# A two-block network in float32 on one core: six edits at waits of TensorE

## The chip, the cores and the metric

The kernel runs on one core of a Trainium2 chip. The metric is the device time of one execution in microseconds, the median over repeated runs. One execution was also taken with the hardware profiler; its rows give the time of every instruction on the five engines: TensorE (PE in the profile; PEld is its weight load), VectorE (DVE), ScalarE (ACT), GpSimd (POOL) and SyncE (SP, which issues most transfers).

## The reference, cut to what matters

The input is 512 tokens of 1024 features. Two hybrid layers come first, then a second block with a state space branch (S5) and a pooling branch, then a final norm. All is float32.

```
def l2norm(t):
    return tf * rsqrt(sum(tf * tf, -1) + EPS)              # q and k of the delta net, 8 heads of 128

# one hybrid layer
h = rmsnorm(x, pre_mix_g);  proj = h @ w_in                # splits: dn_q,k,v,z,b,a, sw_q,k,v, gate_a, gate_b
o = gated_delta_rule(l2norm(q) / sqrt(128), l2norm(k), v, g, beta)   # chunks of 64
y_a = (rmsnorm(o, norm_g) * silu(z)) @ w_up_dn
probs = softmax over a window of 128 keys (with sinks);  o = probs @ v    # 16 query, 2 key/value heads of 64
y_b = o @ w_up_sw
x = x + rmsnorm((sigmoid(gate_a) * y_a + sigmoid(gate_b) * y_b) @ w_o, post_mix_g)
ff = square(relu(rmsnorm(x, pre_mlp_g) @ w_ff1)) @ w_ff2   # 1024 -> 4096 -> 1024
x = x + rmsnorm(ff, post_mlp_g)

# S5 branch of the second block: 32 groups of 16 channels, 64 complex states
dt = exp(log_dt);  abar = exp(lam * dt);  bbar = (abar - 1) / lam * b
s_t = abar * s_(t-1) + bbar u_t;  y = re(c s) + d * u
```

## The kernel before

**Products.** A product with a weight matrix takes 128 output features at a time. The weight tile comes from HBM as `raw` (128x8x128, 512 KB), is rounded to a high part `wh` (ScalarE, L221 and L241; GpSimd for some, L239), and VectorE subtracts to get the low part `wl` (L222, L242). The activations are split in the same way (`split`, L333 to L340: names such as xsh and xsl, ah, hh and hl). Each tile is three matmuls per 128 rows of the contraction, high by high, high by low, low by high (`mm3`, L245; the call itself is L78, a transposition L81). A tile of all 512 tokens is 24 such matmuls. `wh` and `wl` have three buffers, `raw` two; `keep` tiles `kw` have their own pool. PSUM tiles are `psm` (three) and `psa` (five).

**Order.** The program is written as generators that are stepped by `hop()` and `rest()`, and a scheduler then orders the instructions of each engine by its own estimate of times; what is given to `keep_in_program_order` stays in the written order. Each engine works through its own list in order, so an instruction that waits holds all behind it. SP's list holds nearly all loads and stores; the two first `tz` tiles of the second block are loaded by ScalarE's queue (L1572).

**Stages of a layer** (layer 0 in the profile's time, layer 1 some 980 us later). Projections, the convolution and sliding attention, up to 240 us: `sw_item` (L927) exponentiates the scores, transposes them, ScalarE copies them to `pc` (L1007), GpSimd makes two masked copies, `pv` for the block before and `pc` for the own block (L1010, L1012), and TensorE multiplies each by its block of `vt`. The delta net, to 470 us; `norms` (L634) squares four heads of q or k (`sqk`) and TensorE sums over the 128 features of a head, with the squares as the stationary operand and one column of ones moving. The gates and the two up projections, 470 to 580 us (L1303 to L1350): per tile n, `ogf` and two or three gates are fetched from HBM into one ring of three tiles, tag "fe" (L1313); VectorE multiplies ogf by gate 0 (L1335), splits it to `ah`, and multiplies the product of the up projection by gate 2 into `tb` (L1340). `w_o`, to 635 us. FF, 635 to 950 us, in four groups of 1024 hidden features: `relu2` (L1377) makes ft, fq, hh and hl from PSUM or, for the tiles that `fast_pair` forms, from y; `ssm_tables` (L1046) is stepped beside it and makes the S5 tables: it loads `row`, `dt`, `lbr`, `lbi` and `crow` in small pieces (L1059 to L1105). The last group's down projection (L1479 to L1490) works on half the tokens at a time and keeps its last five weights as `kw`.

**Second block,** from 2000 us: TensorE transposes u, ScalarE copies it to `uab` (L1585), TensorE transposes again for `u_g`; then `xv` (L1607), a complex product, scan and complex product on VectorE (L1029 to L1034, L1612) to `sv`, and the products that read sv with `wt`.

Of the kernel before, what the change touches and what calls it, by code (L numbers as in the profile page):

```python
# [9 lines left out]
F32 = mybir.dt.float32  # L10
# [4 lines left out]
ALU = mybir.AluOpType  # L15
# [4 lines left out]
P = 128  # L20
SEQ = 512
D = 1024
NB = SEQ // P
KD = D // P
# [10 lines left out]
EPS = 1e-6  # L35
# [19 lines left out]
def body(  # L55
# [10 lines left out]
    V, S, G, DMA = nc.vector, nc.scalar, nc.gpsimd, nc.sync  # L66
# [33 lines left out]
    def rest(n):  # L100
        for _ in range(n):
            yield
# [17 lines left out]
    def ps_ax(shape=(P, 4, P), name="psa"):  # L120
        return pp.tile(list(shape), F32, tag="ax", name=name, bufs=5)
# [34 lines left out]
    def t2(name, shape=(P, SEQ), dtype=F32):  # L156
        return tp.tile(list(shape), dtype, tag="t2", name=name, bufs=NT2)
# [64 lines left out]
            V.tensor_tensor(out=lo, in0=t, in1=f32(h), op=ALU.subtract)  # L222
            return h, lo

    def load_w(src, kn=KD, n=P, pool_h=False, keep=None):
        turn[0] += 1
        if turn[0] % 3 == 2 and turn[1] is not None and turn[0] > turn[2]:
            raw = turn[1].tile([P, kn, n], F32, tag="rawx", name="rawx", bufs=1)
        else:
            raw = wp.tile([P, kn, n], F32, tag="raw", name="raw", bufs=2)  # L230
        DMA.dma_start(out=raw, in_=src.rearrange("(k p) n -> p k n", p=P))
        h = lo = None
        if keep is not None:
            h, lo = keep(kn, n), keep(kn, n)
        if h is None:
            h = wp.tile([P, kn, n], F32R, tag="wh", name="wh", bufs=3)
            lo = wp.tile([P, kn, n], F32R, tag="wl", name="wl", bufs=3)
        if pool_h:
            G.tensor_scalar(out=h, in0=raw, scalar1=1.0, scalar2=0.0, op0=ALU.mult, op1=ALU.add)  # L239
        else:  # L240
            S.copy(out=h, in_=raw)  # L241
        V.tensor_tensor(out=lo, in0=raw, in1=f32(h), op=ALU.subtract)  # L242
        return h, lo

# [359 lines left out]
    class Quad:  # L604
# [29 lines left out]
        def norms(s, src):  # L634
            sq = [t2("sqk") for _ in range(4)]
            for hh in range(4):
                S.activation(out=sq[hh], in_=src[:, hh].rearrange("p b t -> p (b t)"), func=AF.Square)
            yield from rest(NRM)
            ps = ps_ax((P, NB, 4))
            for hh in range(4):  # L640
                for b in range(NB):
                    T.matmul(ps[:, b, hh:hh + 1], lhsT=sq[hh][:, b * P:(b + 1) * P], rhs=ones[:, 0:1], start=True, stop=True)
                if hh == 1:
                    yield
            ss = small((P, NB, 4), "ss", 2)
            V.tensor_scalar(out=ss, in0=ps, scalar1=EPS, scalar2=None, op0=ALU.add)
            nr = small((P, NB, 4), "nr", 2)
            G.tensor_tensor(out=nr, in0=ss, in1=mhalf.rearrange("p (b h) -> p b h", h=4), op=ALU.pow)
            return ss, nr
# [277 lines left out]
    def sw_item(l, b, kv, qk, vt, sw, kts, db):  # L927
# [70 lines left out]
        V.reciprocal(out=den, in_=den)  # L998
        V.tensor_tensor(out=sc, in0=sc, in1=den.unsqueeze(3).to_broadcast([P, 2, 4, P]), op=ALU.mult)
        yield from rest(PRB)  # L1000
        pcs = []
        for o in range(2):
            ps = ps_ax()
            for i in range(4):
                T.transpose(ps[:, i, :], sc[:, o, i, :], ident)
            pc, pv = sw.tile([P, 4, P], F32, tag="pc", name="pc", bufs=2), None
            S.copy(out=pc, in_=ps)  # L1007
            if b:
                pv = sw.tile([P, 4, P], F32, tag="pv", name="pv", bufs=2)
                G.affine_select(out=pv, in_=pc, pattern=[[0, 4], [-1, P]], base=0, channel_multiplier=1,  # L1010
                                compare_op=ALU.is_gt, fill=0.0)
            G.affine_select(out=pc, in_=pc, pattern=[[0, 4], [1, P]], base=0, channel_multiplier=-1,  # L1012
                            compare_op=ALU.is_ge, fill=0.0)
            pcs.append((pc, pv))
        yield from rest(PV)
        po = ps_ax()
        for o, (pc, pv) in enumerate(pcs):
            hs = slice(64 * o, 64 * o + 64)
            dst = po[hs].rearrange("p h t -> p (h t)")
            if b:  # L1020
                T.matmul(dst, lhsT=vt[:, b - 1, kv * 64:kv * 64 + 64], rhs=pv.rearrange("p h t -> p (h t)"), start=True, stop=False)
            T.matmul(dst, lhsT=vt[:, b, kv * 64:kv * 64 + 64], rhs=pc.rearrange("p h t -> p (h t)"), start=not b, stop=True)
        of = r2("sof")
        V.tensor_copy(out=of, in_=po)
        DMA.dma_start(out=db[:, 4 * kv:4 * kv + 4, b * P:(b + 1) * P], in_=of)
# [20 lines left out]
    def ssm_tables(sp, hf):  # L1046
# [6 lines left out]

        prs = slice(NG * hf, NG * hf + NG)
        grs = slice(2 * NG * hf, 2 * NG * hf + 2 * NG)
        lam = {}
        for nm, src in (("lr", ssm_lam_re_2), ("li", ssm_lam_im_2)):
            row = sp.tile([NG, P], F32, tag="row", name="row")
            DMA.dma_start(out=row, in_=src[0, grs].rearrange("(i two) p -> i (two p)", two=2))  # L1059
            ps = ps_ax((P, NG))  # L1060
            T.transpose(ps, row, ident[:NG, :NG])
            lam[nm] = tl(nm)
            V.tensor_copy(out=lam[nm], in_=ps)
        lr, li = lam["lr"], lam["li"]
        dt = tl("dt")
        for half in range(2):
            DMA.dma_start(out=dt[64 * half:64 * half + 64, :],
                          in_=ssm_log_dt_2[0, grs].rearrange("(i two) -> two i", two=2)[half].partition_broadcast(64))
        bre, bim = tl("lbr", (P, NG, 2, 16))[:, :, 0, :], tl("lbi", (P, NG, 2, 16))[:, :, 0, :]
        for dst, src in ((bre, ssm_b_re_2), (bim, ssm_b_im_2)):  # L1070
            for half in range(2):
                DMA.dma_start(out=dst[64 * half:64 * half + 64],
                              in_=src[0, grs].rearrange("(i two) p c -> two p i c", two=2)[half])
        yield

# [26 lines left out]
        for src in (ssm_c_re_2, ssm_c_im_2):  # L1102
            crow = sp.tile([P, 2, 2, 64], F32, tag="crow", name="crow", bufs=2)
            for dup in range(2):
                DMA.dma_start(out=crow[:, :, dup, :], in_=src[0, grs].rearrange("(q g) c p -> (g c) q p", q=2))  # L1105
            crows.append(crow)
        s16 = (P, NG, 16)
        tC, tD = tl("tC", s16), tl("tD", s16)
# [83 lines left out]
    def layer(l, st, nxt):  # L1192
# [111 lines left out]
        with sbuf(f"mx{l}") as mp:  # L1304
# [8 lines left out]
            def fetch(src, n, name):  # L1313
                t = mp.tile([P, SEQ], F32, tag="fe", name=name, bufs=3)
                DMA.dma_start(out=t, in_=src[:, n, :])
                return t

            def gate(i, n):
                t = fetch(dg[i], n, "gate")
                if (i, n) in plain:  # L1320
                    S.activation(out=t, in_=t, func=gate_fn[i])
                return t
# [47 lines left out]
        with sbuf(f"ff{l}") as ff, ExitStack() as es2:  # L1370
# [17 lines left out]
            def down(g, n):  # L1388
                return w_ff2[l][g * D:(g + 1) * D, n * P:(n + 1) * P], False
# [90 lines left out]
            for i in range(2):  # L1480
                fs = Stats(tr)
                for n in range(KD):
                    if i == 0 and n == 0:
                        wk = {j: w.take() for j in range(3)}
                        head = halves3([wk[j] for j in range(3)], i)
                    elif i == 0 and n >= 3:
                        wk[n] = load_w(down(3, n)[0], keep=keep)
                    ps = head[n] if i == 0 and n < 3 else dense_half(wk[n], hid, i)
                    ac = acc[n][:, HALVES[i]]
                    V.tensor_tensor(out=ac, in0=ps, in1=ac, op=ALU.add)  # L1490
                    fs.add(ac)
                    if i:
                        tick()

                def ff_rstd(i=i, fs=fs):
                    fm = small((P, 2), "fm")
                    V.scalar_tensor_tensor(out=fm, in0=fs.sums(), scalar=1.0 / D, in1=rs4[i], op0=ALU.mult, op1=ALU.mult)
                    V.tensor_scalar(out=fm, in0=fm, scalar1=EPS, scalar2=None, op0=ALU.add)
                    fr = power(fm, 2)
                    V.tensor_tensor(out=fr, in0=fr, in1=rs2[i], op=ALU.mult)  # L1500
                    return fr

                pending = residual(mid, acc, ff_rstd, "post_mlp", l * KD, xst, i)
                if i == 0:
                    before = pending
                    tick = ticks(before, AT_D)
# [52 lines left out]
    with sbuf("ss") as sp:  # L1559
# [20 lines left out]
        for c in range(4):  # L1580
            for j4 in range(2):
                ps = ps_ax((64, 4, P))
                for j in range(4):
                    T.transpose(ps[:, j, :], ua[:, c, 4 * j4 + j::8], ident)
                S.copy(out=uag[:, 8 * c:8 * c + 8, 4 * j4:4 * j4 + 4, :], in_=ps.rearrange("p j (g c) -> p g j c", c=16))  # L1585
        u_g = k8("u_g").rearrange("p a b -> p (a b)").rearrange("p (g b) -> p g b", g=32)
        for g8 in range(4):
            ps = ps_ax((P, 8, 64))
# [180 lines left out]
```

## Time and profile before

| | us |
|---|---|
| median of 3 runs | 2309.17 (2308.73 to 2314.07) |
| the profiled execution | 2315.69 |
| its span from first to last instruction | 2313.9 |
| TensorE busy | 2243.0 (97%) |
| VectorE busy | 1485.3 (64%) |
| ScalarE busy | 952.1 (41%) |
| GpSimd busy | 609.4 (26%) |
| mean granted clock of TensorE | 0.982 of 2.4 GHz |

The profiled execution is 1.8 us longer than its span and 6.5 us above the median. The busy times overlap, since the engines work side by side. A row of the timeline gives start, length, engine, line, operation, the tile written and the tiles read, and in square brackets how long the engine stood before it and what released it.

### The profile page before, as it was taken

The page shows a single profiled execution, that of the slowest core. Times are in us where ns is not written, and L with a number is a line of the kernel's source. Part 1 is how long each engine was busy: PE and PEld are TensorE (multiplying, and loading weights), DVE is VectorE, ACT ScalarE, POOL GpSimd, SP SyncE. Part 2 cuts the span into 40 slices and gives each one's busy share as a digit, 9 for nine tenths or more (in the row PEclk, how much of TensorE's full clock was granted, in tenths as well). Part 3 has the DMA queues.
Part 4 walks back from the last instruction along what each step waited for, and adds up shares of the span by engine and source line. Part 5 has one row for each costly group of instructions (what it writes and reads, how often), then busy time and mean ns, then how long its engine had stood idle before and what let it go on. Part 6 is the DMA issues. An engine that isn't in the chain of part 4 may idle for free. (4 is left out here: it accounts for less than half of the span.)

```text
span 2313.9 us, 37654 instructions
## 1 busy us (share of the span) xinstructions
PE 2243.0 (97%) x14460; PEld 1954.5 (84%) x14460; DVE 1485.3 (64%) x2958; ACT 952.1 (41%) x1726; POOL 609.4 (26%) x675
## 2 busy tenths in 40 slices
PE   8999999999999999999999999999999999899998
PEld 7867888887989899988678888889898898877788
DVE  5579793445576777665797934465777775435645
ACT  4554333333464354444533333334643444423333
POOL 1643420200336123246333202003351242200001
PEclk9999999999999999999999999999999999999999
DMA  5223424565453433342233345654434334563344
GB/s 177 62 72 87 101 83 128 172 200 160 121 157 92 128 107 98 116 125 58 77 87 88 92 127 182 201 164 126 136 101 118 114 97 123 169 165 117 108 131 146
DMA packets 466431, 284.33 MB, mean 123 GB/s; under 512 B 48502, under 2 KB 440012, under 8 KB 465740
## 3 DMA queue, kind: packets, MB, share of 16 engines
q1 hardware_dynamic: 462544, 280.69, 41.9%
q8 instruction: 114, 1.87, 0.3%
q10 hardware_dynamic: 3708, 1.24, 0.3%
q14 instruction: 65, 0.53, 0.1%
HBM read 235.76 MB, written 46.11 MB: 122 GB/s over the span
## 5 line engine op out<-in xcount | busy, mean ns | idle before, releaser
L78 PE MATMUL psm<-xsh,wh 128*128 128x512 f32 (+1 forms) x1136 | 445.6, 393 | 2.6 <-ACT wh L241 1.6
L78 PE MATMUL psm<-xsl,wh 128*128 128x512 f32 (+1 forms) x1136 | 432.6, 381 | 8.2 <-DVE xsl L342 4.2
L78 PE MATMUL psm<-xsh,wl 128*128 128x512 f32 (+1 forms) x1136 | 431.6, 380 | 0.0
L242 DVE TENSOR_TENSOR wl<-raw,wh 128x1024 fp32r<-128x1024 f32 (+2 forms) x179 | 213.3, 1192 | 89.9 <-ACT wh L241 63.6
L78 PEld LDWEIGHTS psm<-xsh,wh 128*128 128x128 f32 x1136 | 217.6, 192 | 48.4 <-issue 8.6
L78 PEld LDWEIGHTS psm<-xsl,wh 128*128 128x128 f32 x1136 | 218.1, 192 | 45.9 <-DVE xsl L342 5.5
L78 PEld LDWEIGHTS psm<-xsh,wl 128*128 128x128 f32 x1136 | 217.3, 191 | 40.9
L241 ACT CAST wh<-raw 128x1024 fp32r<-128x1024 f32 (+3 forms) x126 | 123.4, 980 | 253.6 <-PE psm L78 218.2
L370 POOL TENSOR_TENSOR sa<-sa,sq 128x256 f32<-128x256 f32 x54 | 51.5, 955 | 665.8 <-ACT sq L365 381.5
L78 PE MATMUL psm<-hh,wh 128*128 128x512 f32 (+1 forms) x480 | 177.1, 375 | 6.4 <-ACT hh L336 6.4
L78 PE MATMUL psm<-hl,wh 128*128 128x512 f32 (+1 forms) x480 | 177.7, 372 | 0.8 <-DVE hl L339 0.8
L78 PE MATMUL psm<-hh,wl 128*128 128x512 f32 (+1 forms) x480 | 176.7, 370 | 0.0
L221 ACT CAST wh<-raw 128x1024 fp32r<-128x1024 f32 x67 | 70.2, 1050 | 127.4 <-PE psm L78 76.2
L221 ACT CAST wh<-raws 128x1024 fp32r<-128x1024 f32 x63 | 66.0, 1047 | 127.9 <-PE psm L78 93.7
L222 DVE TENSOR_TENSOR wl<-raw,wh 128x1024 fp32r<-128x1024 f32 x67 | 97.4, 1454 | 26.0 <-ACT wh L221 23.5
L78 PEld LDWEIGHTS psm<-hh,wh 128*128 128x128 f32 x480 | 90.5, 191 | 22.8 <-ACT hh L336 7.0
L78 PEld LDWEIGHTS psm<-hl,wh 128*128 128x128 f32 x480 | 91.5, 191 | 16.4 <-DVE hl L339 1.3
L78 PEld LDWEIGHTS psm<-hh,wl 128*128 128x128 f32 x480 | 91.6, 191 | 15.1
L222 DVE TENSOR_TENSOR wl<-raws,wh 128x1024 fp32r<-128x1024 f32 x63 | 93.6, 1486 | 13.2 <-ACT wh L221 13.2
L239 POOL TENSOR_SCALAR wh<-raw 128x1024 fp32r<-128x1024 f32 (+1 forms) x53 | 62.9, 1186 | 121.0 <-PE psm L78 104.0
L78 PE MATMUL psm<-ah,wh 128*128 128x512 f32 x256 | 83.0, 405 | 5.2 <-ACT ah L336 5.0
L78 PE MATMUL psa<-xsh,wh 128*128 128x256 f32 x288 | 82.3, 286 | 0.0
(670 smaller groups left out, 5662.5 us busy)
## 6 DMA issues: line engine op xcount, KB each, us to landing
raw<-in_w_in_dram SPq DMA_DIRECT2D x130, 512.0 KB, 3.9
raw<-in_w_ff_dram SPq DMA_DIRECT2D x75, 512.0 KB, 4.1
raws<-in_w_ff_dram SPq DMA_DIRECT2D x51, 512.0 KB, 4.3
gate<-dg SPq DMA_DIRECT2D x48, 256.0 KB, 4.4
rawx<-in_w_in_dram SPq DMA_DIRECT2D x14, 512.0 KB, 4.1
raw<-in_w_up_sw_dram SPq DMA_DIRECT2D x12, 512.0 KB, 5.0
raw<-in_w_up_dn_dram SPq DMA_DIRECT2D x11, 512.0 KB, 4.5
raw<-in_w_o_dram SPq DMA_DIRECT2D x10, 512.0 KB, 4.7
```

The costliest lines, as they stand in the source:

```text
L78: return s.issue(nc.tensor.matmul(*a, **k))
L221: S.copy(out=h, in_=t)
L222: V.tensor_tensor(out=lo, in0=t, in1=f32(h), op=ALU.subtract)
L239: G.tensor_scalar(out=h, in0=raw, scalar1=1.0, scalar2=0.0, op0=ALU.mult, op1=ALU.add)
L241: S.copy(out=h, in_=raw)
L242: V.tensor_tensor(out=lo, in0=raw, in1=f32(h), op=ALU.subtract)
L370: (G if s.n in POOL_ACC else V).tensor_tensor(out=s.acc, in0=s.acc, in1=sq, op=ALU.add)
```

## The change

Six places are edited.

1. `load_w` can pin its ScalarE cast to the written order. The last FF group loads kw of tiles 3 and 4 ahead of the first products, pinned, and then, at tile n, that of n + 4.
2. `norms`: the four squares are the moving operand (512 columns) and 32 columns of ones the stationary one; head hh writes partitions 32 hh to 32 hh + 31 of one PSUM tile. ScalarE copies the tile to `sqr`, four transposes follow, and VectorE reads every 32nd column.
3. `sw_item`: p·v is formed as p·v_before + masked(p)·(v_own - v_before). VectorE makes the difference vd; GpSimd makes one masked copy for each o instead of two, none in block 0.
4. `ssm_tables`: its loads keep the written order among the pinned instructions.
5. Gate 2 has a tile ring of its own.
6. The copies to `uab` are made by VectorE.

```diff
@@ -222,7 +222,7 @@
 
-    def load_w(src, kn=KD, n=P, pool_h=False, keep=None):
+    def load_w(src, kn=KD, n=P, pool_h=False, keep=None, pin=False):
         turn[0] += 1
@@ -238,7 +238,9 @@
         else:
-            S.copy(out=h, in_=raw)
+            i = S.copy(out=h, in_=raw)
+            if pin:
+                tc.keep_in_program_order(i)
         V.tensor_tensor(out=lo, in0=raw, in1=f32(h), op=ALU.subtract)
@@ -636,14 +638,17 @@
             yield from rest(NRM)
-            ps = ps_ax((P, NB, 4))
+            pr = ps_ax((P, SEQ))
             for hh in range(4):
-                for b in range(NB):
-                    T.matmul(ps[:, b, hh:hh + 1], lhsT=sq[hh][:, b * P:(b + 1) * P], rhs=ones[:, 0:1], start=True, stop=True)
-                if hh == 1:
-                    yield
+                T.matmul(pr[32 * hh:32 * hh + 32, :], lhsT=ones[:, 0:32], rhs=sq[hh], start=True, stop=True)
+            rows = t2("sqr")
+            S.copy(out=rows, in_=pr)
+            yield
+            ps = ps_ax()
+            for b in range(NB):
+                T.transpose(ps[:, b, :], rows[:, b * P:(b + 1) * P], ident)
             ss = small((P, NB, 4), "ss", 2)
-            V.tensor_scalar(out=ss, in0=ps, scalar1=EPS, scalar2=None, op0=ALU.add)
+            V.tensor_scalar(out=ss, in0=ps[:, :, 0::32], scalar1=EPS, scalar2=None, op0=ALU.add)
             nr = small((P, NB, 4), "nr", 2)
@@ -998,6 +1003,9 @@
         yield from rest(PRB)
+        if b:
+            vd = sw.tile([P, 64], F32, tag="vd", name="vd", bufs=2)
+            V.tensor_tensor(out=vd, in0=vt[:, b, kv * 64:kv * 64 + 64], in1=vt[:, b - 1, kv * 64:kv * 64 + 64], op=ALU.subtract)
         pcs = []
@@ -1007,19 +1015,21 @@
                 pv = sw.tile([P, 4, P], F32, tag="pv", name="pv", bufs=2)
-                G.affine_select(out=pv, in_=pc, pattern=[[0, 4], [-1, P]], base=0, channel_multiplier=1,
-                                compare_op=ALU.is_gt, fill=0.0)
-            G.affine_select(out=pc, in_=pc, pattern=[[0, 4], [1, P]], base=0, channel_multiplier=-1,
-                            compare_op=ALU.is_ge, fill=0.0)
+                G.affine_select(out=pv, in_=pc, pattern=[[0, 4], [1, P]], base=0, channel_multiplier=-1,
+                                compare_op=ALU.is_ge, fill=0.0)
             pcs.append((pc, pv))
...
             dst = po[hs].rearrange("p h t -> p (h t)")
+            pr = pc.rearrange("p h t -> p (h t)")
+            vs = slice(kv * 64, kv * 64 + 64)
             if b:
-                T.matmul(dst, lhsT=vt[:, b - 1, kv * 64:kv * 64 + 64], rhs=pv.rearrange("p h t -> p (h t)"), start=True, stop=False)
-            T.matmul(dst, lhsT=vt[:, b, kv * 64:kv * 64 + 64], rhs=pc.rearrange("p h t -> p (h t)"), start=not b, stop=True)
+                T.matmul(dst, lhsT=vt[:, b - 1, vs], rhs=pr, start=True, stop=False)
+                T.matmul(dst, lhsT=vd, rhs=pv.rearrange("p h t -> p (h t)"), start=False, stop=True)
+            else:
+                T.matmul(dst, lhsT=vt[:, b, vs], rhs=pr, start=True, stop=True)
         of = r2("sof")
@@ -1053,10 +1063,13 @@
         grs = slice(2 * NG * hf, 2 * NG * hf + 2 * NG)
+        def queue(**k):
+            tc.keep_in_program_order(DMA.dma_start(**k))
+
         lam = {}
...
             row = sp.tile([NG, P], F32, tag="row", name="row")
-            DMA.dma_start(out=row, in_=src[0, grs].rearrange("(i two) p -> i (two p)", two=2))
+            queue(out=row, in_=src[0, grs].rearrange("(i two) p -> i (two p)", two=2))
             ps = ps_ax((P, NG))
@@ -1064,12 +1077,12 @@
         for half in range(2):
-            DMA.dma_start(out=dt[64 * half:64 * half + 64, :],
+            queue(out=dt[64 * half:64 * half + 64, :],
                           in_=ssm_log_dt_2[0, grs].rearrange("(i two) -> two i", two=2)[half].partition_broadcast(64))
...
             for half in range(2):
-                DMA.dma_start(out=dst[64 * half:64 * half + 64],
+                queue(out=dst[64 * half:64 * half + 64],
                               in_=src[0, grs].rearrange("(i two) p c -> two p i c", two=2)[half])
@@ -1102,7 +1115,7 @@
             for dup in range(2):
-                DMA.dma_start(out=crow[:, :, dup, :], in_=src[0, grs].rearrange("(q g) c p -> (g c) q p", q=2))
+                queue(out=crow[:, :, dup, :], in_=src[0, grs].rearrange("(q g) c p -> (g c) q p", q=2))
             crows.append(crow)
@@ -1316,7 +1329,11 @@
             def gate(i, n):
-                t = fetch(dg[i], n, "gate")
+                if i == 2:
+                    t = t2("gate2")
+                    DMA.dma_start(out=t, in_=dg[i][:, n, :])
+                else:
+                    t = fetch(dg[i], n, "gate")
                 if (i, n) in plain:
@@ -1482,9 +1499,11 @@
                         wk = {j: w.take() for j in range(3)}
+                        for j in (3, 4):
+                            wk[j] = load_w(down(3, j)[0], keep=keep, pin=True)
                         head = halves3([wk[j] for j in range(3)], i)
-                    elif i == 0 and n >= 3:
-                        wk[n] = load_w(down(3, n)[0], keep=keep)
+                    elif i == 0 and n + 4 < KD:
+                        wk[n + 4] = load_w(down(3, n + 4)[0], keep=keep)
                     ps = head[n] if i == 0 and n < 3 else dense_half(wk[n], hid, i)
@@ -1582,7 +1601,7 @@
                     T.transpose(ps[:, j, :], ua[:, c, 4 * j4 + j::8], ident)
-                S.copy(out=uag[:, 8 * c:8 * c + 8, 4 * j4:4 * j4 + 4, :], in_=ps.rearrange("p j (g c) -> p g j c", c=16))
+                V.tensor_copy(out=uag[:, 8 * c:8 * c + 8, 4 * j4:4 * j4 + 4, :], in_=ps.rearrange("p j (g c) -> p g j c", c=16))
         u_g = k8("u_g").rearrange("p a b -> p (a b)").rearrange("p (g b) -> p g b", g=32)
...
             ps = ps_ax((P, 8, 64))
```

**ScalarE, end of FF in layer 1.** Before, up to the first square of the sums (ft, fq and hh are the steps of one hidden tile, kw the weights kept, wh another weight):

```order
L241 CAST kw<-raw 128x1024
L1380 ACTIVATE ft<-y_19689 128x512
L241 CAST kw<-raw 128x1024
L1382 ACTIVATE fq<-ft 128x512
L1380 ACTIVATE ft<-y_19688 128x512
L241 CAST kw<-raw 128x1024
L336 CAST hh<-fq 128x512
L1382 ACTIVATE fq<-ft 128x512
L336 CAST hh<-fq 128x512
L241 CAST kw<-raw 128x1024
L241 CAST kw<-rawx 128x1024
L365 ACTIVATE sa<-acc 128x256
```

And now:

```order
L1397 ACTIVATE ft<-y_19661 128x512
L1399 ACTIVATE fq<-ft 128x512
L1397 ACTIVATE ft<-y_19660 128x512
L338 CAST hh<-fq 128x512
L1399 ACTIVATE fq<-ft 128x512
L338 CAST hh<-fq 128x512
L241 CAST kw<-raw 128x1024 x2
L367 ACTIVATE sa<-acc 128x256
L367 ACTIVATE sq<-acc 128x256 x2
L241 CAST kw<-raw 128x1024
L367 ACTIVATE sq<-acc 128x256
L241 CAST kw<-raw 128x1024
```

The casts of kw stood between the steps of the two last hidden tiles; now the two tiles' steps stand together, two casts follow them, and the others stand among the squares.

**SP, start of FF in layer 0.** Before (row, dt, lbr, lbi and crow are loads of the S5 tables, raw from in_w_ff the weights, xd_mid and xo the residual's stores and loads):

```order
L1059 DMA row<-in_ssm_lam_re_dram 8x128
L1067 DMA dt<-in_ssm_log_dt_dram 64x8x1 x2
L1072 DMA lbr<-in_ssm_b_re_dram 64x8x16
L231 DMA raw<-in_w_ff_dram 128x8x128
L1072 DMA lbr<-in_ssm_b_re_dram 64x8x16
L1072 DMA lbi<-in_ssm_b_im_dram 64x8x16
L189 DMA raw<-in_w_ff_dram 128x8x128
L1072 DMA lbi<-in_ssm_b_im_dram 64x8x16
L1105 DMA crow<-in_ssm_c_re_dram 128x2x64 x2
L1105 DMA crow<-in_ssm_c_im_dram 128x2x64 x2
L401 DMA xd_mid_5569<-rt 128x256
L430 DMA xo<-xd_in 128x256
```

Now the stretch that holds most of these loads stands further on:

```order
L189 DMA raws<-in_w_ff_dram 128x8x128 x2
L1067 DMA row<-in_ssm_lam_re_dram 8x128
L189 DMA raw<-in_w_ff_dram 128x8x128 x3
L321 DMA tsa<-xd_mid_5555 128x512
L321 DMA tsb<-xd_mid_5555 128x512
L321 DMA tsa<-xd_mid_5555 128x512
L321 DMA tsb<-xd_mid_5555 128x512
L1067 DMA row<-in_ssm_lam_im_dram 8x128
L1067 DMA dt<-in_ssm_log_dt_dram 64x8x1 x2
L1067 DMA lbr<-in_ssm_b_re_dram 64x8x16 x2
L1067 DMA lbi<-in_ssm_b_im_dram 64x8x16 x2
L189 DMA raws<-in_w_ff_dram 128x8x128 x2
```

The weights and the residual that stood behind dt, lbr and lbi have gone ahead of them, and two loads of later weights stand behind them.

**SP, the gates in layer 0.** Before (each row with its tile's number; dg00 and dg02 are gate 0 and gate 2, og0 the delta net's output):

```order
L1315 DMA ogf_5009<-og0_199 128x512
L231 DMA raw_5173<-in_w_up_sw_dram 128x8x128
L1315 DMA gate_5011<-dg00_201 128x512
L1315 DMA gate_5042<-dg02_203 128x512
L1315 DMA ogf_5051<-og0_199 128x512
L231 DMA raw_5215<-in_w_up_sw_dram 128x8x128
L1315 DMA gate_5053<-dg00_201 128x512
L1315 DMA gate_5084<-dg02_203 128x512
L1315 DMA ogf_5094<-og0_199 128x512
```

And now the same tiles:

```order
L1328 DMA ogf_5037<-og0_199 128x512
L1334 DMA gate2_4941<-dg02_203 128x512
L1334 DMA gate2_4984<-dg02_203 128x512
L1334 DMA gate2_5028<-dg02_203 128x512
L1231 DMA dg00_201<-gt__4848 128x512
L231 DMA rawx_5116<-in_w_up_sw_dram 128x8x128
L1334 DMA gate2_5070<-dg02_203 128x512
L1334 DMA gate2_5113<-dg02_203 128x512
L231 DMA raw_5159<-in_w_up_sw_dram 128x8x128
L1328 DMA gate_5039<-dg00_201 128x512
L1328 DMA ogf_5080<-og0_199 128x512
L1334 DMA gate2_5155<-dg02_203 128x512
```

Of each round three loads went into one ring; now two do, and the loads of gate 2 stand on their own.

## Rows read from the trace of the kernel before

**Rows 1.** The page's first part: busy us, share of span, instructions.

```profile
PE 2243.0 (97%) x14460; PEld 1954.5 (84%) x14460; DVE 1485.3 (64%) x2958; ACT 952.1 (41%) x1726; POOL 609.4 (26%) x675
```

**Rows 2.** TensorE's waits: waiter, releaser, us in total, times, longest.

```profile
PE psm L78 <- ACT hh L336: 6.4, 2, 4.4
PE psa L78 <- POOL pv L1010: 6.3, 2, 3.2
PE psm L78 <- ACT ft L1380: 5.4, 2, 2.7
PE psm L78 <- ACT ah L336: 5.0, 2, 2.8
PE psm L78 <- DVE xsl L342: 4.2, 5, 1.3
```

**Rows 3.** Stretches: length, engines' busy us, PEclk, DMA share, GB/s.

```profile
136.40:139.80 3.40, 3.40 (x7) 0.66 (x4) 0.34 (x2) 0.00 (x0) 1.34 (x2) 0.51 0.00 0
528.90:535.70 6.80, 6.41 (x14) 4.76 (x15) 5.54 (x7) 2.95 (x4) 0.00 (x0) 0.50 0.74 227
1610.90:1617.70 6.80, 6.14 (x29) 6.14 (x29) 6.45 (x11) 6.07 (x18) 4.24 (x5) 0.50 0.76 186
945.30:952.10 6.80, 5.35 (x23) 5.05 (x24) 4.25 (x7) 2.97 (x6) 0.73 (x1) 0.50 0.53 153
```

**Rows 4.** Timeline of sliding attention, layer 0: ScalarE, then GpSimd.

```profile
132.64 1.04 ACT L1007 COPY pc<-psa 128x512 f32<-128x512 f32 x2
...
133.27 2.24 POOL L1010 TENSOR_SCALAR_AFFINE_SELECT pv<-pc 128x512 f32<-128x512 f32 x2 [4.37 <-ACT pc L1007]
135.46 1.22 POOL L1012 TENSOR_SCALAR_AFFINE_SELECT pc<-pc 128x512 f32<-128x512 f32 x2
```

**Rows 5.** Timeline of VectorE in the gates, layer 0.

```profile
522.03 0.75 DVE L1335 SCALAR_TENSOR_TENSOR ogf<-ogf,prm,gate 128x512 f32<-128x512 f32 x1 [3.28 <-DMA gate<-dg]
...
524.08 0.69 DVE L1340 TENSOR_TENSOR tb<-psm,gate 128x512 f32<-128x512 f32 x1
```

**Rows 6.** Timeline at FF's start, layer 0: SP's issues, ScalarE, VectorE.

```profile
617.77 0.69 SPq L1067 DMA_DIRECT2D dt<-in_ssm_log_dt_dram  x1
...
630.59 2.85 SPq L1072 DMA_DIRECT2D lbi<-in_ssm_b_im_dram  x1
...
669.88 0.31 SPq L1059 DMA_DIRECT2D row<-in_ssm_lam_im_dram  x1
...
633.02 1.04 ACT L241 CAST kw<-raw 128x1024 fp32r<-128x1024 f32 x1 [10.42 <-DMA raw<-in_w_ff_dram]
...
692.07 1.05 ACT L221 CAST wh<-raws 128x1024 fp32r<-128x1024 f32 x1 [4.38 <-PE psm L78]
...
684.70 0.28 DVE L1033 TENSOR_TENSOR B<-cor,lbi 128x128 f32<-128x128 f32 x1
```

**Rows 7.** The chain that ended last, layer 1: start us, us, what.

```profile
1598.53 11.63 DMA raw<-in_w_ff_dram
...
1652.85 43.75 PE psm L78 x192
```

**Rows 8.** Timeline of ScalarE in the last FF group, layer 1.

```profile
1917.24 0.63 ACT L1380 ACTIVATE ft<-y 128x512 f32<-128x512 f32 x1 [2.74 <-DVE y L310]
1919.52 1.04 ACT L241 CAST kw<-raw 128x1024 fp32r<-128x1024 f32 x1 [1.64 <-DMA raw<-in_w_ff_dram]
```

**Rows 9.** Timeline of TensorE: transposes, squares, attention's pc (two rows per fp32 matmul).

```profile
176.82 0.66 PE L81 MATMUL psa<-ident,sc 128*128 128x128 f32 x4
177.32 1.84 PE L78 MATMUL psa<-ones,sqk 128*128 128x1 f32 x16
...
100.10 1.08 PE L78 MATMUL psa<-pc,vt__214 128*64 128x512 f32 x4
```

**Rows 10.** Timeline of the second block: ScalarE, then VectorE.

```profile
2050.98 2.51 ACT L1585 COPY uab<-psa 64x512 f32<-64x512 f32 x5 [20.41 <-DMA tz<-hpad]
...
2071.82 1.23 DVE L1029 TENSOR_TENSOR tR<-rot,xv 128x1024 f32<-128x1024 f32 x1 [0.47 <-ACT xv L1607]
...
2091.26 1.20 DVE L1034 TENSOR_TENSOR sv<-sv,tR 128x1008 f32<-128x1008 f32 x1
```

## The prediction

> **What bounds the kernel now.** The page's first part says that TensorE is busy in 97% of the span [rows 1], so only three things can make the kernel shorter: fewer columns through TensorE, fewer of its idle stretches, fewer stretches at the lower clock. The table of its waits comes next [rows 2]: the reader is to see that no wait is long, and that the long ones come in pairs, once per layer: for hh, pv, ft and ah. Then the table of stretches with the granted clock [rows 3]: behind such a pause the clock stands at 0.50 (1.2 of 2.4 GHz) for 3.4 or 6.8 us. Fifteen such stretches lie in the span, 75 us together, and where TensorE works through one it loses half of its length. A pause so costs its own length and then 1.7 or 3.4 us. Last, for each pause, the timeline of the engine it waits for.
>
> **The parts, one by one.** The sum is made against the profiled execution, 2315.7 us (span 2313.9 and 1.8 us around it), which is 6.5 us above the median 2309.17; the difference is carried over to the median.
>
> **Attention's p·v** (L1000 to L1025). TensorE waits for GpSimd's pv twice, 6.3 us [rows 2], and once 1.0 us for pc; half clock follows for 3.4 us in layer 0 [rows 3] and for 6.8 us in layer 1, 5.1 us lost. 12.4 us are exposed. In layer 0 ScalarE copies both pc from 132.64 on, and GpSimd's four selects then run to 136.68 one behind the other [rows 4]. With the change the first product reads pc as ScalarE wrote it, at about 133.2, and only one select for each o stands ahead of the second: the last is done at about 135.5 instead of 136.7, and the first product is already through. I take 1.6 us and part of the clock in layer 0, the same and the 1.0 us in layer 1: -6, bounds -12 and -2. The twelve differences vd are 128x64 each on VectorE, small beside the rows of 128x512 (0.69 us [rows 5]), and lie ahead of the wait.
>
> **The third gate's own tile** (L1313 to L1322). Exposed are 5.0 us of waits for ah [rows 2] and half clock behind them, 6.8 us in layer 0 [rows 3] and 3.4 us in layer 1: 10.1 us. The cause is a ring of three tiles that ogf and two gates share: tb at 524.08 frees the tile of the next gate, and VectorE had stood 3.28 us for such a gate [rows 5]; the loop turns in about 7 us while TensorE needs 24 matmuls, 5.5 us (192 took 43.75 [rows 7]). With gate2 out of the ring, ogf and gate 0 can be loaded one round earlier, and in the new order ah of the last round stands ahead of the last tb. TensorE then sets the pace. I take -8, bounds -10 and 0.
>
> **The tables' loads** (L1059 to L1105). In layer 0 SP issues them from 617.77 on, ahead of FF weights; the issues alone run to 633.44 [rows 6], and a weight load put between them took 11.63 us in layer 1 [rows 7]. ScalarE waits 10.42 us for that weight in layer 0 [rows 6], holds ft behind it, and TensorE waits for ft, then for xsl (5.4 and 4.2 us [rows 2]); half clock behind these is 6.8 us in layer 1 [rows 3] and 3.4 us at three other places, 8.5 us lost. 18.1 us are exposed. In the new order weights and residuals go first, and the loads of dt, lbr and lbi follow the second row at 669.88 [rows 6]. The issues then keep SP until about 686, and lbi lands at about 688, some 18 us behind dt as before. VectorE wants it at 684.70: it stands about 3.5 us, with a weight's low part queued behind it. The next weights in SP's queue, loaded at 690 instead of 677, are cast at 692.07, where ScalarE was waiting for TensorE, not for data [rows 6]. So the cover is about two microseconds for the weights and one tile (5.5 us) for VectorE. I book 13 of the 18 us as gained and 2 us per layer as lost again: -9, bounds -18 and +8.
>
> The Trainium skill says against this part (DMA: Bandwidth & Descriptors, "Queues, rings and completion order") that each DMA engine takes the descriptors of one queue in ring order. The trace agrees: the weight issued among the small loads is the one that took 11.63 us. By that the delay is moved to whichever load now stands behind; what it would be worth is the first rival below.
>
> **The last FF group** (L1479 to L1490). Waits for hh 6.4 us [rows 2], some 1.5 us of short ones, half clock 6.8 us in layer 0 [rows 3] and as much in layer 1: 14.7 us. In layer 1 ScalarE has y at 1917.24, but kw waits for its load 1.64 us and is cast ahead of the second step, and another behind it [rows 8]; TensorE waits 4.4 us, the longest for hh [rows 2]. In the new order ft, fq, ft, hh, fq, hh run through and the two kw come after. From 1917.2 these six take 3.5 us, hl ends at about 1921.2, and 1.4 us of wait stay. In layer 0 nothing stays. The kw cast later come in time, but closely: in layer 1 the third is due at about 1929 and lands at about 1926.6, with cast and low part 2.2 us. -11, bounds -15 and -4.
>
> **The squares** (L634 to L649), four times. Removed: 16 matmuls of one column; eight took 1.84 us, so 3.7 us [rows 9]. Added: four of 32x512, a copy by ScalarE beside other work, and four transposes. Of the 32x512 the nearest row is the pair pc, two column groups of 64: 1.08 us for both [rows 9]. Four transposes take TensorE from 176.82 to 177.32, 0.5 us [rows 9]. All four products side by side: 1.1 us and 0.5, a gain of 2.1 each. Two by two: 2.2 and 0.5, a gain of 1.0. One by one, at most 1.08 each: 4.8, a loss of 1.1. So -8, -4 or +4.5; I take -6, between the first two, because the row shows groups together.
>
> The Trainium skill (TensorE: Matmul & The Clock Gate, "Part 3: Packing small matmuls — row/col tiling", the measured speedups) has three column tiles of 32 at 2.38 times, four row tiles at 3.07. By an estimate from that page four take 1.4 times one, not once, and the term would be -6.7; no run here shows four.
>
> **u's copies by VectorE** (L1585). ScalarE stands 20.41 us behind its sixteen loads until 2050.98 [rows 10]. Now VectorE makes them at once. But the copies of xv stay on ScalarE, behind the same sixteen loads: VectorE's chain to sv (2071.82 to 2092.46, 20.6 us [rows 10]) can start at about 2056, so sv is ready at 2077. In the new order only 116 matmuls of 512 columns stand between, before 187: at 0.228 us each [rows 7] they last 26 us from about 2042, where u's transposes stand now. TensorE so runs dry at about 2068, idles 7 to 9 us and pays half clock, where it now pauses twice; the 71 that moved behind take 16.2 us from 2077 on, and the first product of sv and those 71 are through at about 2095, 2 to 3 us later than now. +2, bounds -5 and +5.
>
> Sum: -6 - 8 - 9 - 11 - 6 + 2 = -38. 2315.7 - 38 = 2277.7, on the median's scale 2271.
>
> **The rivals.**
> *The delays are moved, not removed.* The tables' loads cost in their new place what they cost now (0 instead of -9), half of the gates' and the last group's gain returns as new short waits with half clock, the squares go two by two: -6 - 4 - 6 - 4 + 2 = -18, 2291. For it: the 3.5 us that VectorE must stand, and the close cast of kw. Against it: ScalarE's free time before 692.07.
> *The scheduler's order defeats the edits*, so that the change does not do what it says: gate2 loads of several rounds stand on SP ahead of the gate that VectorE needs, and kw's casts come in late; with 3 us of attention's gain and 4 of the squares', 5 us lost in the second block and 2 by a wait for kw it is 2309. For it: five gate2 loads indeed stand close together on SP in the new order. Against: the tile each fills is free long before.
> *Slower: VectorE starves TensorE behind lbi.* Place: the wait at 684.70 and its like in layer 1. Price: each microsecond beyond one tile's cover (5.5 us) is one of TensorE's. From -38 it takes 45 us to be clearly slower, 22 us in each layer, so the five small loads would have to take about 42 us instead of 18. With 25 us a layer, 2321. For it: their issues are held up by a full queue already (2.85 us for one [rows 6]). Against: nothing big stands among them any more.
>
> **How the numbers follow.** Forecast (2258 to 2284) 0.55; moved 0.24; gains above the forecast (full exposure of the waits, 2245 to 2258) 0.07; defeated 0.08; slower 0.06. About 0.3%, 7 us, is what a measurement here tells from no change. So faster 0.86, same 0.08, slower 0.06. The range takes the forecast and most of the first rival: 2253 to 2297.
>
> **What would show it.** Right: no wait for ah, hh and ft in TensorE's table, pv under 3 us, fewer than ten stretches at 0.50; `psa<-ones` of the squares within 1.1 us for four; ScalarE without a 10 us wait at FF's start; a wait of VectorE for lbi of 2 to 5 us; TensorE dry once before sv, for 5 to 10 us. Wrong: VectorE's wait for lbi above 10 us with TensorE waiting for wl; matmuls of the squares one behind the other; a new wait for kw.

## The result and the profile after

The changed kernel takes 2273.7 us (2271.2 to 2278.6, four runs) where the kernel before takes 2309.6: the ratio is 0.984, 95% interval 0.982 to 0.986, a gain of 36 us. The profiled execution of the changed kernel is its longest, 2278.6 us with a span of 2276.8, 37.1 us under the span before.

First the page's first part and rows of TensorE's table of waits (waiter, releaser, us in total, times, longest), the answer to [rows 1, 2].

```profile
PE 2216.5 (97%) x14380; PEld 1929.3 (85%) x14380; DVE 1492.5 (66%) x2978; ACT 942.9 (41%) x1718; POOL 591.8 (26%) x643
```

```profile
...
PE psa L78 <- DMA tz<-hpad: 7.1, 1, 7.1
PE psa L78 <- ACT p L789: 4.6, 2, 2.8
...
PE psa L78 <- DVE y L312: 3.3, 2, 1.6
PE psm L78 <- DVE wl L244: 3.2, 4, 2.1
...
PE psa L78 <- POOL pv L1018: 1.3, 2, 0.6
```

The waits for hh, ft and ah are gone, pv is down from 6.3 to 1.3 us. Two that were not in the table before are now among its four longest: tz, and the delta net's p. Of the 37.1 us, 10.6 are idle time of TensorE. Its busy time fell by the other 26.5 us although only the squares took matmuls away: most of that is time at half clock.

The stretches at half clock were fifteen with 75 us; now there are seven with 37 us (one more ends each span, behind the last matmul). Half of the difference, 19 us, is time gained. Three of the seven (length, busy us of each engine, granted clock, DMA share, GB/s), the answer to [rows 3]:

```profile
251.60:255.00 3.40, 3.40 (x9) 2.65 (x8) 1.58 (x3) 0.36 (x1) 0.00 (x0) 0.50 0.00 0
...
1210.80:1217.50 6.70, 5.93 (x58) 4.73 (x58) 3.09 (x5) 1.05 (x3) 0.00 (x0) 0.50 0.26 72
...
2012.90:2019.60 6.70, 3.71 (x14) 2.91 (x15) 4.73 (x7) 4.17 (x6) 0.00 (x0) 0.50 0.96 157
```

The first two stand behind the waits for p, the third behind tz. None is left behind attention, at FF's start or in the last FF group.

To place the gain, the start of the same TensorE instructions was compared in the two traces, at the ends of the stages; the differences of neighbours are what each stage gave (us, negative is faster).

| stage | layer 0 | layer 1 |
|---|---|---|
| sliding attention, with the first sum of squares | -6.5 | -8.6 |
| delta net, with the second sum | +1.1 | +4.9 |
| gates and up projections | -2.8 | -4.1 |
| FF, first group's start | -7.4 | -8.5 |
| FF, the groups between | +1.9 | +1.8 |
| last FF group and layer's end | -4.9 | -5.5 |
| second block | +1.5 | |

They add up to -37. Three rows have the other sign: there the gain was partly given back. Each trace is one execution. The gates' row of layer 0 holds a wait of 2.1 us for the first weights' low part and a stretch at half clock behind it, which no trace of the kernels below has at that place.

The rows of single parts. The last FF group in layer 1, timeline of ScalarE, beside [rows 8]:

```profile
1882.97 0.63 ACT L1397 ACTIVATE ft<-y 128x512 f32<-128x512 f32 x1 [2.55 <-DVE y L312]
...
1885.86 0.62 ACT L338 CAST hh<-fq 128x512 fp32r<-128x512 f32 x1
1886.39 1.99 ACT L241 CAST kw<-raw 128x1024 fp32r<-128x1024 f32 x2
...
1893.88 1.05 ACT L241 CAST kw<-raw 128x1024 fp32r<-128x1024 f32 x1 [3.74 <-DMA raw<-in_w_ff_dram]
```

From y to the last hh it is 3.5 us, as worked out. FF's start in layer 0, timeline of ScalarE, SP and VectorE, beside [rows 6]:

```profile
617.46 1.05 ACT L241 CAST kw<-raw 128x1024 fp32r<-128x1024 f32 x1 [2.90 <-DMA raw<-in_w_ff_dram]
...
654.82 1.37 SPq L1067 DMA_DIRECT2D dt<-in_ssm_log_dt_dram  x2
...
657.87 6.22 SPq L1067 DMA_DIRECT2D lbi<-in_ssm_b_im_dram  x2
...
668.57 0.17 DVE L1091 TENSOR_TENSOR tA<-lr,dt 128x8 f32<-128x8 f32 x1 [4.08 <-ACT dt L1089]
```

ScalarE waits 2.9 instead of 10.4 us. In their new place the issues from dt to lbi keep SP for 9.3 us, not 15.7, and VectorE stands 4.1 us, for dt and not for lbi (3.9 us in layer 1). The squares and their transposes (timeline of TensorE, two rows per fp32 matmul), beside [rows 9]:

```profile
173.83 1.06 PE L78 MATMUL psa<-sqk,ones 128*32 128x512 f32 x8
...
178.69 0.66 PE L81 MATMUL psa<-ident,sqr 128*128 128x128 f32 x4
```

Four column groups of 32 side by side take what two of 64 took. The second block, ScalarE then TensorE, beside [rows 10]:

```profile
2012.12 1.07 ACT L1626 COPY xv<-psa 128x512 f32<-128x512 f32 x2 [20.09 <-DMA tz<-hpad]
...
2015.89 1.12 PE L78 MATMUL psa<-tz,u_g 128*64 128x128 f32 x8 [7.09 <-DMA tz<-hpad]
```

### The profile page after: what moved, and what is told of

The parts are those of the page before. It is cut to its first block, busy times and chain, and to the rows that moved or that the text cites. A ratio compares the mean times of both kernels' runs of the same rounds, so it can differ in the third digit from the quotient of the medians.

```text
span 2276.8 us, 37483 instructions
## 1 busy us (share of the span) xinstructions
PE 2216.5 (97%) x14380; PEld 1929.3 (85%) x14380; DVE 1492.5 (66%) x2978; ACT 942.9 (41%) x1718; POOL 591.8 (26%) x643
## 5 line engine op out<-in xcount | busy, mean ns | idle before, releaser
L78 PE MATMUL psa<-xsl,wh 128*128 128x256 f32 x288 | 81.4, 283 | 0.0
```

Source lines behind the costliest of these rows:

```text
L78: return s.issue(nc.tensor.matmul(*a, **k))
```

## The experiments

Ratios are against runs of the kernel before on the same chip. Their intervals are some 0.0015 to 0.002 on each side, so two kernels compared through them differ with certainty only from about 6 us on; below that the traces have to speak. In six kernels one part is undone in the changed kernel.

**Without the new squares.** (`norms` as before.)

> The changed kernel with the squares summed as before (16 one-column matmuls). Theory A (the gain is given back behind it): each of the four sums is 2.1 us longer again, 8.3 us in all, but TensorE then comes later to the delta net's p and its new wait there (1.8 and 2.8 us, each with half clock behind it) shrinks, so the median is only 2 to 5 us above the changed kernel's 2273.7. Theory B (the wait at p has nothing to do with when TensorE arrives): the waits stay as they are and the whole 8 us is seen, 2282.

Ratio 0.9842 (0.9823 to 0.9860), 2272.4 us: no difference from the changed kernel. The waits for p are gone from TensorE's table, and with them the half clock behind them. Changed kernel first (TensorE, then ScalarE), then this one, both in layer 0:

```profile
244.83 0.69 PE L78 MATMUL psa<-td,na 32*32 32x32 f32 x32
...
250.43 0.21 PE L78 MATMUL psa<-u,p 32*32 32x32 f32 x1 [1.79 <-ACT p L789]
...
247.50 1.91 ACT L632 ACTIVATE qk__2587<-qk__2587 128x2048 f32<-128x2048 f32 x1
...
250.01 0.36 ACT L789 COPY p<-psa 32x256 f32<-32x256 f32 x1
```

```profile
246.69 0.69 PE L78 MATMUL psa<-td,na 32*32 32x32 f32 x32
250.26 0.22 PE L78 MATMUL psa<-u,p 32*32 32x32 f32 x2
...
246.67 1.91 ACT L632 ACTIVATE qk__2592<-qk__2592 128x2048 f32<-128x2048 f32 x1
...
249.19 0.36 ACT L786 COPY p<-psa 32x256 f32<-32x256 f32 x1
```

TensorE comes 1.9 us later to the product that makes p, and the Silu ahead of p's copy starts 0.8 us earlier; with twelve matmuls between, p is then there. So the new squares bring TensorE to a place where ScalarE's list holds it. By the starts of the same TensorE instructions in the two traces, the stretches of the four sums are 9.3 us shorter in the changed kernel, and the two around p 9.4 us longer. Only two of the four sums stand ahead of a p. The 5.5 us that they save are lost there, and 3.9 us more, since half clock follows the waits; the other two sums make up for that. Theory A holds: no gain is seen in this kernel, though the times alone would leave room for some 6 us.

The kernel before had little room at p in layer 0, and more in layer 1 (TensorE, then ScalarE, layer 0 and then layer 1):

```profile
254.76 0.22 PE L78 MATMUL psa<-u,p 32*32 32x32 f32 x2
...
254.33 0.36 ACT L784 COPY p<-psa 32x256 f32<-32x256 f32 x1
```

```profile
1235.65 0.22 PE L78 MATMUL psa<-u,p 32*32 32x32 f32 x2
...
1234.16 0.37 ACT L784 COPY p<-psa 32x256 f32<-32x256 f32 x1
```

The copy ends 0.07 us ahead of TensorE's first use in layer 0, and 1.1 us ahead in layer 1.

**Without vd** (attention's two masked copies as before).

> The changed kernel with attention's two masked copies as before. In the changed kernel's trace the stretch of attention gave 3.8 us in layer 0 and 5.7 in layer 1 besides the squares. Theory A (given back at the delta net's p): with 9.5 us back on, the waits for p and their half clock (3.5 and 6.2 us) vanish in part, and the median is 2 to 6 us above 2273.7. Theory B (independent): 9 to 10 us above, waits for p unchanged.

Ratio 0.9864 (0.9847 to 0.9881), 2276.1 us: 5 us above by the ratios, not apart from zero by itself. In the trace the waits for pv are 6.3 us again, those for p have shrunk from 4.6 to 1.4 us, and no half clock stands behind them: part is given back there, as in theory A.

**Without the loads' fixed order.**

> The changed kernel with the tables' loads in the scheduler's order again. Theory A (the loads delayed the weights, and the change removed that): FF's first group loses 16 us again in the two layers, the late waits for y (1.6 us in each layer) vanish, so 12 us above 2273.7. Theory B (the delay is only moved): not more than 5 us above, because the loads' cost in the new place goes away.

Ratio 0.9897 (0.9879 to 0.9915), 2283.4 us: 12 us above, theory A. The waits for ft are back (5.3 us), and those for y are down from 3.3 to 0.4 us. The delay was not only moved.

**Without gate 2's own ring.**

> The changed kernel with gate 2 in the shared ring again. Theory A (the ring set the pace, and the wait at the first weights of the up projection is only the earlier arrival of TensorE): 10 us are lost at the last ah and the 3.5 us wait at the start of the stretch stays, so 10 us above 2273.7. Theory B (gate 2's loads in SP's list cause that wait): it goes, and the median is 6 to 7 us above.

Ratio 0.9884 (0.9868 to 0.9899), 2281.6 us: 9 us above. The waits for ah are back (4.3 us). The amount is theory A's. But the wait for the first weights' low part, 2.1 us in the changed kernel's trace, is 0.5 us in this one, and lies between nothing and 3.1 us in those of the other kernels with gate 2's own ring; half clock follows it only in the changed kernel's. It belongs to one execution more than to the edit, so that half of theory A isn't shown.

**Without the last group's early weights.**

> The changed kernel with the last FF group's weights loaded as before. Theory A (as booked): 4.9 us in layer 0 and 5.5 in layer 1 are lost again to the wait for hh and the half clock behind it, 10 us above the changed kernel's 2273.7. Theory B (given back at the layer's end, where TensorE waits for the sums anyway): 5 us above or less.

Ratio 0.9901 (0.9884 to 0.9919), 2285.8 us: 13 us above, theory A. It is the largest part by the ratios, but not apart from the tables' loads. The waits for hh are back (6.2 us).

**u's copies by ScalarE again.**

> The changed kernel with u's copies by ScalarE again. Theory A (this edit only changes what TensorE waits for in the second block: 7.1 us for tz instead of 4.6 for the copies): 1 to 2 us below 2273.7, so about 2272. Theory B (the copies were the bound there, and the tz wait comes from elsewhere): 5 us above.

Ratio 0.9834 (0.9818 to 0.9851), 2269.0 us: 2 us below the changed kernel by the ratios, within the noise. In the traces the second block alone is 2.5 us shorter than with VectorE's copies; TensorE no longer waits for tz, but 2.2 us for uab and then 2.7 us for a weight's cast on ScalarE. Theory A in sign and size, by the trace.

**p's second half by VectorE.**

```diff
-                S.copy(out=p1[96:128], in_=pP[96:128])
+                V.tensor_copy(out=p1[96:128], in_=pP[96:128])
```

> The changed kernel with the second half of the delta net's p copied by VectorE (0.4 us) and not by ScalarE, where it stands behind a 1.9 us Silu and a table load. Theory A (that place in ScalarE's list is what gave the squares' gain back): TensorE's waits for p, 4.6 us, and the half clock behind them, 5.1 us lost, go: 6 to 9 us below 2273.7. Theory B (VectorE stands there too, for the same late weights): no change within 2 us.

Ratio 0.9832 (0.9816 to 0.9848), 2268.9 us: 2 to 5 us below, not apart from zero by the ratios. Timeline of VectorE in layer 0:

```profile
247.97 0.42 DVE L788 COPY p<-psa 32x256 f32<-32x256 f32 x1
248.42 0.43 DVE L789 COPY p<-psa 32x256 f32<-32x256 f32 x1
```

Both halves follow each other at once, and there is no wait for p left, nor half clock behind it. But TensorE now waits 2.4 us for t, the next copy of the same chain. So the wait goes as theory A has it, and some of it comes back one step on; the 6 to 9 us are not seen in the times, whose noise doesn't exclude them.

**tz ahead of rot and wt.**

```diff
-            DMA.dma_start(out=rot[i], in_=d_r[i])
-            DMA.dma_start(out=wt[i], in_=d_w[i])
...
                 d = (S if g8 < 2 else DMA).dma_start(out=tz[16 * j:16 * j + 16], in_=...)
+                if g8 >= 2:
+                    tc.keep_in_program_order(d)
+        for i in range(2):
+            tc.keep_in_program_order(DMA.dma_start(out=rot[i], in_=d_r[i]))
+            tc.keep_in_program_order(DMA.dma_start(out=wt[i], in_=d_w[i]))
```

> The changed kernel with SP's sixteen tz loads issued ahead of the loads of rot and wt (3 MB), which are needed later. Theory A (tz waits because it stands behind these bytes): TensorE's 7.1 us wait for tz and 3.4 us of half clock go, but sv bounds next, at most 5 us later than now; 4 to 8 us below 2273.7. Theory B (tz is held by its own many small pieces on two queues): tz lands no earlier, no change within 2 us.

Ratio 0.9810 (0.9794 to 0.9827), 2264.3 us: 8 to 9 us below the changed kernel. In the trace the second block alone is 8.5 us shorter. SP's issues in this kernel, and TensorE's product of sv:

```profile
1986.59 11.81 SPq L1589 DMA_DIRECT2D tz<-hpad  x16
1998.49 0.37 SPq L1593 DMA_DIRECT2D rot<-d_r  x1
...
2029.95 0.44 PE L78 MATMUL psa<-wt,sv 64*64 64x128 f32 x4 [1.18 <-DVE sv L1044]
```

The wait for tz has left the table, and sv costs 1.2 us in its place. Theory A.

**Both of these.**

> The changed kernel with p's second half copied by VectorE and with SP's tz loads ahead of rot and wt. Theory A (the two places are far apart and independent): the gains add, 5 us and 9 us, about 2260. Theory B (they share something, such as the clock or a queue): not below the second alone, 2264.

Ratio 0.9795 (0.9781 to 0.9808), 2260.1 us, theory A's number. In the trace TensorE waits neither for p nor for tz; by the times alone the 3 to 4 us below tz alone are within the noise, so theory B isn't excluded by them. It beats the kernel before by 49 us and the changed kernel by 11 to 14.

**p by VectorE, squares as before.**

> The changed kernel with p's second half copied by VectorE, but the squares summed as before. Theory A (the squares' gain is real once the wait for p is out of the way): 6 to 8 us above the same kernel with the new squares (2268.9), so 2275 to 2277. Theory B (the new squares bring nothing in any case, because other waits of the delta net take their place): within 2 us of 2268.9.

Ratio 0.9845 (0.9831 to 0.9858), 2272.9 us, 3 to 4 us above the same with the new squares: between the theories, and not apart from either of them.

**The squares alone in the kernel before.**

> The kernel before with only the squares changed. There p's second half is ready only 0.07 us before TensorE needs it. Theory A (given back at p): waits for p of about 2 us with half clock behind them, so not more than 4 us below the kernel before. Theory B (the squares' gain is seen when it stands alone): 8 us below.

Ratio 0.9981 (0.9969 to 0.9993): 4 us below the kernel before, between 2 and 7. Theory B's 8 us lie outside the interval, theory A's limit of 4 us within. But its waits of 2 us are not there: one wait for p appears, 1.0 us in layer 0, and no half clock behind it. By the starts of the same instructions each of the four sums is 1.9 us shorter, and around the places of p 2.0 us come back in layer 0 and 1.1 in layer 1. So 4.6 of 7.7 us stay, close to the 4 us of the ratio.

**p by VectorE, tz ahead, u's copies by ScalarE.**

> The changed kernel with p's second half copied by VectorE, tz loads ahead, and u's copies by ScalarE. Theory A (u's copies by VectorE cost 2.5 us only because of the tz wait, which is gone): this is 5 us or more slower than with VectorE, because ScalarE's copies again stand behind its own sixteen tz loads, about 2265. Theory B (the copies by VectorE cost in any case): 2 us faster, about 2258.

Ratio 0.9788 (0.9772 to 0.9803), 2259.4 us, against 0.9795 with VectorE's copies: no difference beyond the noise. Theory A's 5 us are not there. Theory B's 2 us the times can't tell from nothing, but in the traces the second block differs by less than 0.1 us. So once tz stands ahead, u's copies by VectorE neither help nor cost: in neither table does TensorE wait for uab or tz, and for sv at most 0.2 us.

## Why the prediction was right

The sum was -38, measured is -36. It is that near partly by luck: the squares' 6 us did not come, and the tables' loads and the last group brought about as much more than booked. Term by term, with what the undone part cost in the experiments (difference of the ratios times 2309 us, each to about 6 us):

| part | booked | undone |
|---|---|---|
| attention's p·v | -6 | -5 |
| gate 2 | -8 | -9 |
| tables' loads | -9 | -12 |
| last FF group | -11 | -13 |
| squares | -6 | 0 |
| u's copies | +2 | +2 |

The single rows are no surer than their 6 us; the traces carry the account below.

Attention: the sum holds, but by two errors that cancel. By the stages of the traces the edit gave more (15.1 us with the first sums of squares, which are 4 us of it), and part of it went at p.

Gates and last group: right in place and size. The working of the last group (3.5 us from y to the last hh, kw in time but closely) is in the rows nearly as put; the third kw's load was there 10.9 us behind y, not 9.4, and TensorE waited 0.8 us for a kw, a small case of the new wait for kw that the prediction had put among the signs of being wrong.

Tables' loads: the gain at FF's start was 15.9 us where 13 were booked, and 3.7 us were lost again in the groups between, where 4 were booked. The mechanism of the loss is another: VectorE waited for dt, once in each layer, and not for lbi; with no large loads among them the small ones were issued in 9.3 us, where 15.7 had been carried over. The 3.7 us appear some 60 us later as waits for y; without the fixed order nearly all of these go, but what carries the delay there was not followed.

Squares: the step that failed. The direct price was right, and better than booked: four abreast, 1.1 us and 0.5 in place of 3.7, 8 us in all. The failure is the unwritten step behind it, that time taken from TensorE there is time taken from the kernel. In the kernel before, p was ready only 0.07 us before TensorE used it in layer 0 and 1.1 us in layer 1, which its trace shows and the prediction did not look for. Of what attention and the squares gave, p and the half clock behind it took back 9.4 us. With the rest of the change the squares' 8 us come to nothing that can be measured, and alone, or with p copied by VectorE, to some 3 to 4 us (the second not apart from nothing).

u's copies: right in sum by luck, wrong in mechanism. TensorE did not run dry for want of sv; it waited 7.1 us for tz, which its list had ahead of the remaining matmuls, and this wait happens to have the size booked for the other (7 to 9 us). I had followed VectorE's chain and not the second operand.

Of the rivals, the moved delay describes the squares and part of attention's gain. The slower one had no part: VectorE's wait was 4.1 us, and by its own working it would have begun beyond 5.5.

## What to carry to other kernels

When one engine is busy throughout, an edit's gain is the pause it removes plus the clock that the pause costs, and it holds only as far as the next engine's margin at the following join: look there for copies that end just in time (here 0.07 us in one layer, 1.1 in the other) before booking it. Ahead of a join list every operand, loads too, and ask which lands last once the one you repair is early. Small scattered loads belong behind the weights that are needed next.

## What the runs showed of the hardware

Four fp32 matmuls of 32 stationary and 512 moving columns, in four column groups, take 1.06 us together, as two of 64 do (1.08 us, [rows 9]).

A VectorE subtraction of 128x1024, 1.22 us where GpSimd does nothing, took 3.11 us in the changed kernel beside two GpSimd multiplies of 128x512, in either layer (layer 0; VectorE, then GpSimd):

```profile
237.15 3.11 DVE L244 TENSOR_TENSOR wl<-raw,wh 128x1024 fp32r<-128x1024 f32 x1 [0.99 <-POOL wh L239]
...
237.15 1.03 POOL L663 TENSOR_TENSOR tg<-tri,gh 128x512 fp32r<-128x512 f32 x1
238.15 1.03 POOL L663 TENSOR_TENSOR tg<-tri,dc 128x512 fp32r<-128x512 f32 x1
```

The taps ahead of the Silu stand behind that subtraction, so this may be part of why p comes late there; no run took it apart.
